# Experts' sigmoid bank and copies, layer norm sums asked two units later, last merge block on VectorE by halves

## The chip, the cores and the metric

One core of a Trainium2 chip runs the program. Its engines work side by side, each through its own queue of instructions in a fixed order: TensorE (PE, with its weight loads shown apart as PEld), VectorE (DVE), ScalarE (ACT), GpSimd (POOL) and SyncE (SP), which issues the transfers. The metric is the device time of one execution in microseconds.

## What is computed

One decoder block on 256 tokens of 1024 channels: a merge of a convolution branch and a gated linear recurrence (HGRN2), then a mixture of 32 experts of which each token takes four. Cut to what matters:

```python
mod = silu(c) @ w_ada + b_ada                       # six sections: sh1, sc1, ga1, sh2, sc2, ga2
h = rmsnorm(x, g_mix) * (1 + sc1) + sh1
p = h @ w_in                                        # 8192 columns: a, b, q, f, i, g, gc, gh
u = causal_depthwise_conv31(a * sigmoid(b)) + bias
y_conv = silu(layernorm(u, ln_g, ln_b)) @ w_conv_out
y_hg = (rmsnorm(hgrn2_scan(q, f, i)) * silu(g)) @ w_hgrn_out
merged = sigmoid(gc) * y_conv + sigmoid(gh) * y_hg
x = x + ga1 * (merged @ w_out)
h2 = rmsnorm(x, g_ffn) * (1 + sc2) + sh2
gl, lin = split(h2[tokens of e] @ w1[e] + b1[e])    # top-4 of 32 experts by the router
y = (min(gl, 7) * sigmoid(1.702 * min(gl, 7)) * (clip(lin, -7, 7) + 1)) @ w2[e] + b2[e]
out = rmsnorm(x + ga2 * sum(top_w * y), g_final)
```

## The kernel before

**Products.** The four dense products run as 44 units of 256 output columns: units 0 to 31 for w_in, 32 to 35 for w_ho (`ho_ps`), 36 to 39 for w_co (`co_ps`), 40 to 43 for w_wo (`wo_ps`). Each is 48 matmuls of 256 columns: every factor is split in a high part (rounded to the fast type) and a low part (the rest), and three of the four products are added. `split_half` (L378) makes the parts of a unit's weights in two halves of 128x1024, one unit ahead: the high part is a cast on ACT (L393), the low part a subtraction on POOL or DVE (L395, chosen by the tables SPLIT_DVE and SPLIT_HALF). Unit 31's low parts are DVE's, unit 41's are POOL's.

**Order around the units.** The loop at L711 issues unit after unit and hands out other work between them: the convolution's taps on DVE (`conv_taps`, L460, counts in the table TAPS), sections of `mod` on PE (L343, after the units in MOD_AT; a section ends in a copy to `mods` on ACT, L348), the norm of the recurrence (`oss`, `orr`, `ors`, `sg`, `o`, with casts of `sg` at L632), and the layer norm. A scheduler puts the instructions in the engines' queues. At unit LN_FROM = 23 the rest of the taps is issued and the layer norm begins; each later unit takes it a step further. Its steps: column sums `mup` of `cv` on PE (L255), copied to `mus`, totalled as `mu` (L264); `cv` minus mean on DVE (L565), squares `csq` on ACT (L569), sums `varp` (L571), copied to `vars`, totalled as `var`; reciprocal root `rv` on ACT and DVE (L229, L230), the product of `cv` with it on DVE (L579); then for 256-column pieces a sigmoid (`sigy`, L586) and an affine operation (L587) on ACT and a product on DVE (L589). In the traces a unit's matmuls are the rows `p_ps<-h,ws`, 48 of them.

**Gated merge** (L799 to L814). For each of four blocks of w_co: `tm` = `co_ps` times one gate, plus the other gate's term (both DVE, 128x512), a high part by a copy on ACT (L810), a low part by a subtraction on DVE (L811). The results `mg` are factors of w_wo's units, which start right behind.

**Experts** (L1004 on). The weights come in 1 MB loads (`w_w`) into 22 slots, issued by SP in order, each when its slot is free. An expert holds up to 64 tokens: `gather` multiplies them out into the bank `xg_ps` (L983; two experts at a time, so before every second one), `first_layer` fills the banks `u_gl` and `u_lin` (L1019, 32 matmuls of 512 columns), then gl is clamped on DVE (L1026), its sigmoid is taken on ACT (L1027), lin is clamped (L1028), and two products follow (L1029, L1030). `turn` transposes the result into the bank `ta` (L1043) and copies it out on ACT (L1045), `second_layer` multiplies by w2 into `yp` (L1058), and the results are added to `acc` (L1079). An expert with more than 64 tokens also takes a path for 32 more (`small_first`, `small_second`) behind a branch; in this input only expert 25 does. The last expert works by halves.

Of the kernel before, what the change touches and what calls it, by code (L numbers as in the profile page):

```python
# [9 lines left out]
F32 = mybir.dt.float32  # L10
# [4 lines left out]
ALU = mybir.AluOpType  # L15
PSUM = bass.MemoryType.PSUM

P = 128
# [12 lines left out]
LIMIT = 7.0  # L31
# [9 lines left out]
MOD_EXTRA = {}  # L41
LOADS = (18, 0, 0, 1, 0, 0, 1, 0, 0, 1, 0, 0, 0, 0, 1, 2, 2, 2, 2, 0, 0, 1, 0, 0, 1, 1, 0, 0, 1, 0, 0, 1, 1, 0, 0, 1, 0, 0, 0, 0, 0, 0, 0, 0, 0, 1, 0, 0, 0, 1, 1, 0, 0, 0, 0, 0, 0, 1, 1, 0, 0, 1, 1, 0, 0, 1, 0, 0, 0, 0, 0, 0, 1, 0, 0, 1, 1, 0, 0, 1, 0, 0, 0, 0, 0, 1, 0, 0, 1, 1, 0, 0, 1, 1, 2, 0, 0, 0, 0, 3, 1, 0, 0, 1, 1, 0, 0, 1, 1, 3, 0, 0, 0, 0, 0, 0, 0, 0, 0, 1, 1, 1, 0, 1, 1, 2, 0, 0, 1, 0, 0, 1, 0, 0, 1, 0, 0, 1, 1, 0, 0, 0, 0, 0, 1, 1, 0, 0, 0, 0, 1, 1, 2, 1, 0, 0, 1, 0, 0, 1, 0)
TAPS = (1, 0, 0, 0, 5, 4, 10, 6, 5, 5, 13, 6, 16, 14, 17, 11, 5, 8, 0, 6, 0, 0, 0, 0, 0, 3, 13, 9, 17, 15, 9, 5)
LN_FROM = 23
SPLIT_DVE = (3, 4, 6, 28, 29, 30, 31, 37, 38, 40, 42)
SPLIT_HALF = (4, 6, 17, 19, 21, 25, 27, 28, 32, 34, 35, 36, 40, 42, 43)
E_RUN = E
# [43 lines left out]
def block_kernel(ctx, tc, xT_d, x_d, prm_d, con_d, wada0_d, wada_d, bada_d, gfin_d, win_d, wco_d, who_d, wo_d,  # L91
                 wr_d, br_d, w1_d, b12_d, w2_d, out_d):
    nc = tc.nc
# [346 lines left out]
    def step(jobs, n):  # L440
        while n > 0 and jobs:
            try:
                next(jobs[0])
                n -= 1
            except StopIteration:
                jobs.pop(0)
# [263 lines left out]
    taps, lv0, lv1, norms, lns = [], [], [], [], []  # L710
    mods = [mod_section(j) for j in SECTIONS]  # L711
    for n, b in enumerate(IN_ORDER):
        part, i = divmod(b, 4)
        cs = slice(2 * i, 2 * i + 2)
        ps = early[n] if n < N_EARLY else block_product(n, hx, "p_ps", part == 4, n == 31)
# [54 lines left out]
        if n in MOD_AT:  # L770
            step(mods, 1)
        elif n > MOD_AT[0]:
            step(mods, MOD_EXTRA.get(n, 0))
        if n == LN_FROM:
            step(taps, 1000)
            lns.append(layer_norm())
        step(lns, 1)
        step(taps, TAPS[n])
# [6 lines left out]
    def gate(b, j):  # L785
        return gates[b // 2][:, j, b % 2 * 2:b % 2 * 2 + 2, :]

    for b in range(4):
        if b == 3:
            step(lns, 100)  # L790
        ps = block_product(32 + b, ox, "ho_ps", last=b == 3, middle=(lambda: split_y(0)) if b == 3 else None)
# [8 lines left out]
    for b in range(4):  # L800
        ps = block_product(36 + b, yx, "co_ps", last=b == 3)
        if b == 2:
            split_half(40, 0)
        if b % 2 == 0:
            mg.append(split_slot(f"mg{b // 2}"))
        tm = temp("tm").rearrange("p (m t) -> p m t", m=2)
        nc.vector.tensor_tensor(out=tm, in0=ps, in1=gate(b, 0), op=ALU.mult)
        nc.vector.tensor_tensor(out=tm, in0=tm, in1=gate(b, 1), op=ALU.add)
        hi, lo = (mg[b // 2][:, j, b % 2 * 2:b % 2 * 2 + 2, :] for j in range(2))
        nc.scalar.copy(out=hi, in_=tm)  # L810
        nc.vector.tensor_tensor(out=lo, in0=tm, in1=hi.bitcast(F32), op=ALU.subtract)  # L811
        if b % 2 == 1:
            free()
        step(preps, 2)  # L814
# [34 lines left out]
    for b in range(3):  # L849
        ps = block_product(40 + b, mg, "wo_ps", True)  # L850
# [8 lines left out]
    ps = bank("wo_ps").rearrange("p (m t) -> p m t", m=2)  # L859
# [38 lines left out]
    lo = of_rt(0, TOP_K + E)  # L898
# [9 lines left out]
    for t in range(NT):  # L908
# [4 lines left out]
                                       op0=ALU.mult, op1=ALU.add)  # L913
# [7 lines left out]
        if t == 1:  # L921
# [3 lines left out]
                                       op0=ALU.add, op1=ALU.mult)  # L925
# [81 lines left out]
    def first_layer(xg, i, w1s, hot, pieces=1):  # L1007

        up = [bank("u_gl"), bank("u_lin")]
        for nb in range(2):  # L1010
            for g in range(2):
                nc.tensor.matmul(up[nb][g * 64:(g + 1) * 64, :], lhsT=hot, rhs=b12[:, nb, g * 512:(g + 1) * 512],  # L1012
                                 start=True, stop=False)
        for kt in range(KT):
            w = w1s(kt)
            for nb in range(2):
                for g in range(2):
                    c = nb * FF + g * 512
                    nc.tensor.matmul(up[nb][g * 64:(g + 1) * 64, :], lhsT=xg[kt // 4][:, kt % 4, i * CAP:(i + 1) * CAP],  # L1019
                                     rhs=w[:, c:c + 512], start=False, stop=kt == KT - 1)  # L1020
        gl = temp("gl")
        li = temp("li")
        si = up[0]
        for c in range(0, 512, 512 // pieces):
            c = slice(c, c + 512 // pieces)
            nc.vector.tensor_scalar(out=gl[:, c], in0=up[0][:, c], scalar1=LIMIT, scalar2=None, op0=ALU.min)  # L1026
            nc.scalar.activation(si[:, c], gl[:, c], AF.Sigmoid, scale=ALPHA)  # L1027
            nc.vector.tensor_scalar(out=li[:, c], in0=up[1][:, c], scalar1=LIMIT, scalar2=-LIMIT, op0=ALU.min, op1=ALU.max)  # L1028
            nc.vector.scalar_tensor_tensor(out=li[:, c], in0=li[:, c], scalar=1.0, in1=gl[:, c], op0=ALU.add, op1=ALU.mult)  # L1029
            nc.vector.tensor_tensor(out=li[:, c], in0=li[:, c], in1=si[:, c], op=ALU.mult)  # L1030
        return li
# [6 lines left out]
    def turn(li, at_, pieces=1, piece=0):  # L1038
        ta = bank("ta")
        n = 4 // pieces  # L1040
        for j in range(piece * n, (piece + 1) * n):
            c = pick_columns(li, j) if pieces == 1 else li[:, j * P:(j + 1) * P]
            nc.tensor.transpose(ta[:, j * P:(j + 1) * P], c, ident)  # L1043
        c = slice(piece * n * P, (piece + 1) * n * P)
        nc.scalar.copy(out=at_[:, c], in_=ta[:, c])  # L1045

    def second_layer(at_, w2s, hot):
        aT = at_.rearrange("p (j g s) -> p j g s", j=4, g=2)
# [42 lines left out]
    def small_first(o, places, weights, hot, w1s, at_, owt, a, b, ps, u):  # L1091
# [17 lines left out]
        def out_of(src):  # L1109
            nc.scalar.copy(out=a[:, halves[0]], in_=src[:, halves[0]])  # L1110
            nc.vector.tensor_copy(a[:, halves[1]], src[:, halves[1]])

        out_of(ps)
        for t in range(NT):
            nc.vector.tensor_scalar(out=ow[:, t * SMALL:(t + 1) * SMALL], in0=iota[:, 0:SMALL], scalar1=places[t],
                                    scalar2=weights[t], op0=ALU.is_equal, op1=ALU.mult)
# [152 lines left out]
    for e in range(E_RUN):  # L1269
# [48 lines left out]
        at_ = li  # L1318
# [164 lines left out]
```

## Time and profile before

| | |
|---|---|
| median of 3 runs | 1324.36 us (1322.4 to 1326.33) |
| the profiled execution | 1321.67 us, its span 1319.9 us |
| PE busy | 1219.9 us, 92% of the span |
| DVE, ACT, POOL busy | 545.2, 286.5, 163.4 us |
| mean granted TensorE clock | 0.983 |
| read from HBM | 477.11 MB, 362 GB/s over the span |
| stages, from the PE timeline | w_in to 290.83, w_ho from 294.01, w_wo from 343.58, expert 0 at 384.04, expert 24 at 1068.54, expert 31 at 1282.30 |

All numbers of the trace come from the one profiled execution, in microseconds from its span's start. In a row of a timeline stand the start, the busy time, engine, line, operation, output <- inputs, the shape and the number of instructions drawn together; a bracket at the end gives the idle time of that engine just before and what ended it. "issue" is time in which the engine waited for nothing that the profile shows. PEclk is the granted clock as a share of 2.4 GHz.

### The profile page before, as it was taken

The numbers are of one execution on the slowest core, as the hardware profiler recorded it, in microseconds if no ns is written. First come the engines' busy times: TensorE is split into PE (matmuls) and PEld (weight loads), VectorE is DVE, ScalarE is ACT, GpSimd is POOL, SyncE is SP. The second block draws the span as 40 slices with busy tenths as digits, with TensorE's granted clock in tenths as the row PEclk, the third lists the DMA queues.
The fourth block names the chain that finished last, engine by engine and source line by source line (L and its number), as shares of the span: only waits on it lengthen the run. The fifth ranks groups of instructions, "written<-read, shape, count | busy, mean of one in ns | idle before, by whom it ended". The sixth has DMA issues, their size and how long they took to land. (4 is left out here: it accounts for less than half of the span.)

```text
span 1319.9 us, 19185 instructions
## 1 busy us (share of the span) xinstructions
PE 1219.9 (92%) x7829; PEld 669.9 (51%) x7829; DVE 545.2 (41%) x1121; ACT 286.5 (22%) x449; POOL 163.4 (12%) x78
## 2 busy tenths in 40 slices
PE   7999998999899999999999889988888898999997
PEld 6899788779864343443434333332323243434432
DVE  4498996545644242332323223232222232323322
ACT  4445444664720010001000000100000000100112
POOL 3258665222300000000000000000000000000000
PEclk9999989999999999999999899999999998999999
DMA  9993335656689999999999999999999999999995
GB/s 381 410 406 130 130 129 198 235 205 236 255 324 410 421 410 419 420 420 419 421 420 421 421 419 421 420 420 420 421 420 418 420 421 419 421 403 420 420 419 202
DMA packets 71399, 480.02 MB, mean 364 GB/s; under 512 B 7521, under 2 KB 8801, under 8 KB 15970
## 3 DMA queue, kind: packets, MB, share of 16 engines
q1 hardware_dynamic: 70834, 477.47, 88.5%
q8 instruction: 91, 1.49, 0.5%
q10 hardware_dynamic: 432, 0.72, 0.2%
q14 instruction: 42, 0.34, 0.1%
HBM read 477.11 MB, written 1.05 MB: 362 GB/s over the span
## 5 line engine op out<-in xcount | busy, mean ns | idle before, releaser
L1019 PE MATMUL u_gl<-w_w,xg 128*64 128x512 f32 x1024 | 270.1, 599 | 23.6 <-DMA w_w<-in_w_dram 23.6
L1019 PE MATMUL u_lin<-w_w,xg 128*64 128x512 f32 x1024 | 266.8, 592 | 0.0
L1058 PE MATMUL yp<-w_w,li 128*64 128x512 f32 x992 | 227.2, 606 | 19.1 <-ACT li L1045 10.5
L1019 PEld LDWEIGHTS u_gl<-w_w,xg 128*64 128x64 f32 x1024 | 75.9, 137 | 165.1 <-issue 88.8
L1026 DVE TENSOR_SCALAR gl<-u_gl 128x512 f32<-128x512 f32 (+1 forms) x33 | 22.3, 675 | 329.1 <-PE u_gl L1019 321.2
L1019 PEld LDWEIGHTS u_lin<-w_w,xg 128*64 128x64 f32 x1024 | 80.6, 137 | 140.0 <-issue 139.9
L1058 PEld LDWEIGHTS yp<-w_w,li 128*64 128x64 f32 x992 | 71.7, 139 | 156.5 <-issue 133.9
L409 PEld LDWEIGHTS p_ps<-h,ws 128*128 128x128 f32 x1152 | 141.4, 194 | 12.1 <-issue 5.9
L409 PE MATMUL p_ps<-h,ws 128*128 128x256 f32 x1152 | 146.2, 287 | 0.0
L1068 DVE TENSOR_TENSOR yg<-yp,ga 64x512 f32<-64x512 f32 x60 | 41.3, 689 | 225.6 <-PE yp L1058 225.0
L395 POOL TENSOR_TENSOR ws<-w_in,ws 128x1024 fp32r<-128x1024 f32 x45 | 113.1, 2527 | 87.2 <-ACT ws L393 77.8
L1276 POOL PARTITION_BROADCAST w_gfin<-w_gfin x1 | 1.3, 1305 | 898.6 <-DMA w_w<-in_w_dram 898.6
L1027 ACT ACTIVATE u_gl<-gl 128x512 f32<-128x512 f32 (+1 forms) x33 | 19.4, 589 | 427.2 <-DVE gl L1026 427.2
L460 DVE SCALAR_TENSOR_TENSOR cv<-u,pre,cv 128x229 f32<-128x229 f32 (+28 forms) x240 | 95.2, 456 | 8.6 <-ACT cv L457 7.9
L983 PE MATMUL xg_ps<-o,w_x 128*128 128x128 f32 (+1 forms) x544 | 65.4, 278 | 13.5 <-DVE li L1028 10.3
L1071 ACT ACTIVATE ys0h<-yg,by 64x512 fp32r<-64x512 f32 x30 | 21.6, 720 | 254.0 <-DVE yg L1068 254.0
L393 ACT CAST ws<-w_in 128x1024 fp32r<-128x1024 f32 x64 | 65.7, 1047 | 46.7 <-PE p_ps L409 17.6
L983 PEld LDWEIGHTS xg_ps<-o,w_x 128*128 128x128 f32 x544 | 62.2, 192 | 26.6 <-DVE li L1028 21.7
L987 DVE TENSOR_SCALAR xg<-xg_ps,g,sh 128x128 f32<-128x128 f32 (+1 forms) x136 | 45.3, 396 | 16.5 <-PE xg_ps L983 11.6
L1045 ACT COPY li<-ta 128x512 f32<-128x512 f32 (+1 forms) x33 | 18.9, 573 | 114.6 <-PE ta L1043 109.2
L395 DVE TENSOR_TENSOR ws<-w_in,ws 128x1024 fp32r<-128x1024 f32 x19 | 27.1, 1439 | 11.2 <-ACT ws L393 11.2
L409 PE MATMUL wo_ps<-ws,mg 128*128 128x256 f32 x192 | 26.0, 295 | 2.7 <-DVE mg L811 2.0
(292 smaller groups left out, 1158.1 us busy)
## 6 DMA issues: line engine op xcount, KB each, us to landing
w_w<-in_w_dram SPq DMA_DIRECT2D x380, 1024.0 KB, 19.9
w_in<-in_win_dram SPq DMA_DIRECT2D x32, 1024.0 KB, 11.0
w_ada<-in_wada_dram SPq DMA_DIRECT2D x24, 1024.0 KB, 16.3
w_ho<-in_who_dram SPq DMA_DIRECT2D x4, 1024.0 KB, 8.2
w_co<-in_wco_dram SPq DMA_DIRECT2D x4, 1024.0 KB, 8.4
w_wo<-in_wo_dram SPq DMA_DIRECT2D x4, 1024.0 KB, 9.6
w_w<-in_w_dram SPq DMA_DIRECT2D x8, 512.0 KB, 15.2
xT<-in_xT_dram SPq DMA_DIRECT2D x1, 1024.0 KB, 6.9
```

The source lines that it names most:

```text
L393: nc.scalar.copy(out=to[:, 0], in_=w[:, ks, :])
L395: (nc.vector if dve else nc.gpsimd).tensor_tensor(out=to[:, 1], in0=w[:, ks, :], in1=to[:, 0].bitcast(F32), op=ALU.subtract)
L409: nc.tensor.matmul(out, lhsT=lt, rhs=rh, start=first and kt == 0 and i == 0, stop=kt == KT - 1 and i == 2, skip_group_check=not first)
L460: nc.vector.scalar_tensor_tensor(out=cv[:, ct, s:], in0=u[i][:, m, :T - s], scalar=tap, in1=cv[:, ct, s:], op0=ALU.mult, op1=ALU.add)
L983: nc.tensor.matmul(ps[:, i, cs], lhsT=x2[:, t, kt * P:(kt + 1) * P], rhs=o[:, 0, t, cs], start=t == 0, stop=t == NT - 1)
L987: nc.vector.tensor_scalar(out=xg[h][:, i, cs], in0=ps[:, i, cs], scalar1=g2[:, kt:kt + 1], scalar2=sh2[:, kt:kt + 1], op0=ALU.mult, op1=AL ...
L1019: nc.tensor.matmul(up[nb][g * 64:(g + 1) * 64, :], lhsT=xg[kt // 4][:, kt % 4, i * CAP:(i + 1) * CAP], rhs=w[:, c:c + 512], start=False, s ...
L1026: nc.vector.tensor_scalar(out=gl[:, c], in0=up[0][:, c], scalar1=LIMIT, scalar2=None, op0=ALU.min)
L1027: nc.scalar.activation(si[:, c], gl[:, c], AF.Sigmoid, scale=ALPHA)
L1058: nc.tensor.matmul(yp[g * 64:(g + 1) * 64, :], lhsT=aT[:, kt % 4, kt // 4, :], rhs=w[:, kk, g * 512:(g + 1) * 512], start=False, stop=kt = ...
L1068: nc.vector.tensor_tensor(out=y[rows, :], in0=yp[gs, :], in1=ga2[gs, :], op=ALU.mult)
L1071: nc.scalar.activation(hi[rows, :], y[rows, :], AF.Copy, scale=by[rows, :])
```

## The change

Three independent parts. First, a constant TAPS_END = 23 keeps the place at which the taps are issued, and LN_FROM moves from 23 to 25, so that the layer norm's steps are asked two units later. Second, the fourth block of the gated merge is done in two halves of 256 columns, and its high part is copied by DVE; the other blocks stay. Third, in the experts: the sigmoid is written to the bank of `u_lin` in place of that of `u_gl`, with lin's clamp issued ahead of it; the copy out of `ta` is two copies of 256 columns; and the first copy of `small_first` is one copy of 512 columns on ACT in place of one half on ACT and one on DVE.

```diff
@@ -41,7 +41,8 @@
-LN_FROM = 23
+TAPS_END = 23
+LN_FROM = 25
 SPLIT_DVE = (3, 4, 6, 28, 29, 30, 31, 37, 38, 40, 42)
 SPLIT_HALF = (4, 6, 17, 19, 21, 25, 27, 28, 32, 34, 35, 36, 40, 42, 43)
 E_RUN = E
@@ -771,8 +772,9 @@
             step(mods, 1)
         elif n > MOD_AT[0]:
             step(mods, MOD_EXTRA.get(n, 0))
+        if n == TAPS_END:
+            step(taps, 1000)
         if n == LN_FROM:
-            step(taps, 1000)
             lns.append(layer_norm())
         step(lns, 1)
         step(taps, TAPS[n])
@@ -804,11 +806,16 @@
         if b % 2 == 0:
             mg.append(split_slot(f"mg{b // 2}"))
         tm = temp("tm").rearrange("p (m t) -> p m t", m=2)
-        nc.vector.tensor_tensor(out=tm, in0=ps, in1=gate(b, 0), op=ALU.mult)
-        nc.vector.tensor_tensor(out=tm, in0=tm, in1=gate(b, 1), op=ALU.add)
         hi, lo = (mg[b // 2][:, j, b % 2 * 2:b % 2 * 2 + 2, :] for j in range(2))
-        nc.scalar.copy(out=hi, in_=tm)
-        nc.vector.tensor_tensor(out=lo, in0=tm, in1=hi.bitcast(F32), op=ALU.subtract)
+
+        for m in (slice(0, 1), slice(1, 2)) if b == 3 else (slice(0, 2),):
+            nc.vector.tensor_tensor(out=tm[:, m], in0=ps[:, m], in1=gate(b, 0)[:, m], op=ALU.mult)
+            nc.vector.tensor_tensor(out=tm[:, m], in0=tm[:, m], in1=gate(b, 1)[:, m], op=ALU.add)
+            if b == 3:
+                nc.vector.tensor_copy(hi[:, m], tm[:, m])
+            else:
+                nc.scalar.copy(out=hi[:, m], in_=tm[:, m])
+            nc.vector.tensor_tensor(out=lo[:, m], in0=tm[:, m], in1=hi[:, m].bitcast(F32), op=ALU.subtract)
         if b % 2 == 1:
             free()
         step(preps, 2)
@@ -1020,12 +1027,13 @@
                                      rhs=w[:, c:c + 512], start=False, stop=kt == KT - 1)
         gl = temp("gl")
         li = temp("li")
-        si = up[0]
+
+        si = up[1]
         for c in range(0, 512, 512 // pieces):
             c = slice(c, c + 512 // pieces)
             nc.vector.tensor_scalar(out=gl[:, c], in0=up[0][:, c], scalar1=LIMIT, scalar2=None, op0=ALU.min)
+            nc.vector.tensor_scalar(out=li[:, c], in0=up[1][:, c], scalar1=LIMIT, scalar2=-LIMIT, op0=ALU.min, op1=ALU.max)
             nc.scalar.activation(si[:, c], gl[:, c], AF.Sigmoid, scale=ALPHA)
-            nc.vector.tensor_scalar(out=li[:, c], in0=up[1][:, c], scalar1=LIMIT, scalar2=-LIMIT, op0=ALU.min, op1=ALU.max)
             nc.vector.scalar_tensor_tensor(out=li[:, c], in0=li[:, c], scalar=1.0, in1=gl[:, c], op0=ALU.add, op1=ALU.mult)
             nc.vector.tensor_tensor(out=li[:, c], in0=li[:, c], in1=si[:, c], op=ALU.mult)
         return li
@@ -1041,8 +1049,10 @@
         for j in range(piece * n, (piece + 1) * n):
             c = pick_columns(li, j) if pieces == 1 else li[:, j * P:(j + 1) * P]
             nc.tensor.transpose(ta[:, j * P:(j + 1) * P], c, ident)
-        c = slice(piece * n * P, (piece + 1) * n * P)
-        nc.scalar.copy(out=at_[:, c], in_=ta[:, c])
+
+        for j in range(piece * n, (piece + 1) * n, 2):
+            c = slice(j * P, (j + 2) * P)
+            nc.scalar.copy(out=at_[:, c], in_=ta[:, c])
 
     def second_layer(at_, w2s, hot):
         aT = at_.rearrange("p (j g s) -> p j g s", j=4, g=2)
@@ -1110,7 +1120,8 @@
             nc.scalar.copy(out=a[:, halves[0]], in_=src[:, halves[0]])
             nc.vector.tensor_copy(a[:, halves[1]], src[:, halves[1]])
 
-        out_of(ps)
+
+        nc.scalar.copy(out=a, in_=ps)
         for t in range(NT):
             nc.vector.tensor_scalar(out=ow[:, t * SMALL:(t + 1) * SMALL], in0=iota[:, 0:SMALL], scalar1=places[t],
                                     scalar2=weights[t], op0=ALU.is_equal, op1=ALU.mult)
```

Lines of the changed kernel are up to ten further down: L255 is L256, L586 is L587, L811 is L818, L1045 is L1055.

PE's queue around units 24 to 27, before: `p_ps` rows are the units (two rows each), `ob` belongs to the recurrence, `mod` to the modulation.

```order
L609 MATMUL ob<-at_1164,v 128x128
L255 MATMUL mup<-cv,pre 32x256 x8
L409 MATMUL p_ps<-h_150,ws 128x256 x24
L409 MATMUL p_ps<-h_151,ws 128x256 x24
L607 MATMUL ob<-at_1164,v 128x256
L609 MATMUL ob<-at_1164,v 128x128
L607 MATMUL ob<-at_1164,v 128x256
L609 MATMUL ob<-at_1164,v 128x128
L264 MATMUL mu<-mus,con 128x256
L409 MATMUL p_ps<-h_150,ws 128x256 x24
L409 MATMUL p_ps<-h_151,ws 128x256 x24
```

After, units 24 to 26 and the start of 27:

```order
L410 MATMUL p_ps<-h_150,ws 128x256 x24
L410 MATMUL p_ps<-h_151,ws 128x256 x24
L608 MATMUL ob<-at_1682,v 128x256
L610 MATMUL ob<-at_1682,v 128x128
L608 MATMUL ob<-at_1682,v 128x256
L610 MATMUL ob<-at_1682,v 128x128
L344 MATMUL mod_2112<-w_ada_2_2057,pre 32x512 x4
L256 MATMUL mup<-cv,pre 32x256 x8
L410 MATMUL p_ps<-h_150,ws 128x256 x24
L410 MATMUL p_ps<-h_151,ws 128x256 x24
L608 MATMUL ob<-at_1682,v 128x256
L610 MATMUL ob<-at_1682,v 128x128
```

`mup` stood ahead of unit 24 and stands ahead of unit 26; `mu`, ahead of unit 25 before, now stands ahead of unit 27 (behind the last rows shown). Likewise `varp` moves from unit 26 into unit 28 and `var` from ahead of unit 27 to ahead of unit 29, and the last two sections of `mod`, which stood ahead of and behind unit 31, both stand ahead of it.

ACT's queue ahead of unit 31, before; `w_in_2762` is the weight of unit 30, `w_in_2808` that of unit 31, `gates` rows close a unit, `o_3195` are the casts of `sg`.

```order
L586 ACTIVATE sigy<-cv,pre 128x256 x2
L587 ACTIVATE cv<-cv,pre 128x256 x2
L586 ACTIVATE sigy<-cv,pre 128x256 x2
L587 ACTIVATE cv<-cv,pre 128x256 x2
L374 COPY ga_181<-bb 128x512
L764 ACTIVATE gates<-p_ps 128x512
L632 CAST o_3124<-sg 128x512 x2
L393 CAST ws<-w_in_2762 128x1024 x2
L764 ACTIVATE gates<-p_ps 128x512
L632 CAST o_3195<-sg 128x512
L393 CAST ws<-w_in_2808 128x1024
L632 CAST o_3195<-sg 128x512
```

After; `w_in_2793` is the weight of unit 31, `gates` at the top closes unit 29, at the bottom unit 30.

```order
L765 ACTIVATE gates<-p_ps 128x512
L587 ACTIVATE sigy<-cv,pre 128x256 x2
L633 CAST o_3171<-sg 128x512 x2
L588 ACTIVATE cv<-cv,pre 128x256 x2
L587 ACTIVATE sigy<-cv,pre 128x256 x2
L588 ACTIVATE cv<-cv,pre 128x256 x2
L587 ACTIVATE sigy<-cv,pre 128x256 x2
L588 ACTIVATE cv<-cv,pre 128x256 x2
L587 ACTIVATE sigy<-cv,pre 128x256 x2
L588 ACTIVATE cv<-cv,pre 128x256 x2
L394 CAST ws<-w_in_2793 128x1024 x2
L765 ACTIVATE gates<-p_ps 128x512
```

The sixteen operations on `sigy` and `cv` stood ahead of unit 30's casts; now they and two casts of `sg` stand between unit 30's casts and those of unit 31.

DVE's queue at the last block of the merge, before:

```order
L811 TENSOR_TENSOR mg_3807<-tm,mg_3807 128x512
L395 TENSOR_TENSOR ws<-w_wo_3322,ws 128x1024
L807 TENSOR_TENSOR tm<-co_ps,gates 128x512
L808 TENSOR_TENSOR tm<-tm,gates 128x512
L811 TENSOR_TENSOR mg_3807<-tm,mg_3807 128x512
L845 TENSOR_TENSOR tmo<-wo_ps,ga_3331 128x256
L846 TENSOR_TENSOR w_x<-w_x,tmo 128x256
```

After:

```order
L818 TENSOR_TENSOR mg_3807<-tm,mg_3807 128x512
L396 TENSOR_TENSOR ws<-w_wo_3322,ws 128x1024
L812 TENSOR_TENSOR tm<-co_ps,gates 128x256 x2
L813 TENSOR_TENSOR tm<-tm,gates 128x256 x2
L815 CAST mg_3807<-tm 128x256 x2
L818 TENSOR_TENSOR mg_3807<-tm,mg_3807 128x256 x2
L852 TENSOR_TENSOR tmo<-wo_ps,ga_3331 128x256
L853 TENSOR_TENSOR w_x<-w_x,tmo 128x256
```

Three operations of 512 columns became eight of 256, the copy `CAST` among them, which ACT's queue loses. POOL and SP keep their instructions in their order.

## Rows read from the trace of the kernel before

**Rows 1.** The page, GB/s moved in 40 equal slices of the span

```profile
GB/s 381 410 406 130 130 129 198 235 205 236 255 324 410 421 410 419 420 420 419 421 420 421 421 419 421 420 420 420 421 420 418 420 421 419 421 403 420 420 419 202
```

**Rows 2.** Waits of PE weight loads, 410 to 1066 us: total, times, longest

```profile
PEld u_gl L1019 <- DMA w_w<-in_w_dram: 65.2, 58, 1.8
```

**Rows 3.** Timeline of PE, experts 24 and 31

```profile
1083.34 1.08 PE L1019 MATMUL u_gl<-w_w,xg 128*64 128x512 f32 x4 [0.55 <-DMA w_w<-in_w_dram]
...
1093.72 9.36 PE L1058 MATMUL yp<-w_w,li 128*64 128x512 f32 x30 [3.58 <-issue]
...
1296.83 1.03 PE L1019 MATMUL u_gl<-w_w,xg 128*64 128x512 f32 x4
```

**Rows 4.** Windows: busy time (operations) of each engine, granted clock, DMA share, GB/s

```profile
262.10:270.10 8.00, 8.00 (x54) 5.36 (x53) 4.23 (x5) 7.99 (x18) 0.00 (x0) 1.00 0.81 339
350.00:355.00 5.00, 3.73 (x20) 3.74 (x21) 2.37 (x4) 0.28 (x1) 3.44 (x2) 0.66 1.02 431
405.00:410.00 5.00, 4.80 (x24) 1.66 (x26) 0.62 (x2) 0.14 (x1) 0.00 (x0) 1.00 0.94 356
475.00:480.00 5.00, 4.21 (x26) 2.08 (x23) 2.66 (x4) 0.60 (x1) 0.00 (x0) 1.00 0.95 349
1165.00:1170.00 5.00, 4.32 (x21) 2.43 (x21) 2.83 (x7) 1.19 (x2) 0.00 (x0) 1.00 0.80 305
1304.00:1305.00 1.00, 0.87 (x4) 0.30 (x5) 0.00 (x0) 0.85 (x2) 0.00 (x0) 1.00 0.13 49
```

**Rows 5.** Timeline of PE, units 23 to 31

```profile
220.75 0.64 PE L255 MATMUL mup<-cv,pre 128*32 128x256 f32 x2 [3.65 <-DVE cv L460]
221.32 7.46 PE L409 MATMUL p_ps<-h,ws 128*128 128x256 f32 x48
...
239.85 2.09 PE L571 MATMUL varp<-csq,pre 128*32 128x256 f32 x12 [0.44 <-ACT csq L569]
...
251.28 0.70 PE L264 MATMUL var<-vars,con 128*128 128x256 f32 x2
...
292.60 1.98 PE L367 MATMUL gb<-mods,con 128*128 128x512 f32 x4 [0.71 <-ACT mods L348]
```

**Rows 6.** Timeline of ACT, ahead of the unit 30 casts

```profile
270.99 1.14 ACT L632 CAST o<-sg 128x512 fp32r<-128x512 f32 x2
```

**Rows 7.** Timeline of DVE, layer norm

```profile
255.62 2.28 DVE L579 TENSOR_TENSOR cv<-cv,rv 128x2048 f32<-128x2048 f32 x1
257.82 1.22 DVE L395 TENSOR_TENSOR ws<-w_in,ws 128x1024 fp32r<-128x1024 f32 x1
```

**Rows 8.** Timeline of all engines, last block of the merge and w_wo

```profile
342.43 0.69 DVE L811 TENSOR_TENSOR mg<-tm,mg 128x512 fp32r<-128x512 f32 x1
...
343.58 4.48 PE L409 MATMUL wo_ps<-ws,mg 128*128 128x256 f32 x36
...
345.15 0.68 DVE L807 TENSOR_TENSOR tm<-co_ps,gates 128x512 f32<-128x512 f32 x1
...
348.31 5.14 POOL L395 TENSOR_TENSOR ws<-w_wo,ws 128x1024 fp32r<-128x1024 f32 x2 [9.94 <-ACT ws L393]
...
348.78 2.43 DVE L811 TENSOR_TENSOR mg<-tm,mg 128x512 fp32r<-128x512 f32 x1 [2.21 <-ACT mg L810]
...
348.80 0.50 PE L409 MATMUL wo_ps<-ws,mg 128*128 128x256 f32 x2 [0.74 <-ACT mg L810]
...
351.26 8.56 PE L409 MATMUL wo_ps<-ws,mg 128*128 128x256 f32 x58 [1.96 <-DVE mg L811]
```

**Rows 9.** Timelines of PE and ACT, experts 27 and 31

```profile
1191.47 3.84 PE L983 MATMUL xg_ps<-o,w_x 128*128 128x128 f32 x32 [0.78 <-DVE li L1028]
...
1196.68 7.09 PE L1058 MATMUL yp<-w_w,li 128*64 128x512 f32 x32 [0.34 <-ACT li L1045]
...
1196.04 0.59 ACT L1045 COPY li<-ta 128x512 f32<-128x512 f32 x1 [4.85 <-PE ta L1043]
...
1301.37 0.37 ACT L1045 COPY li<-ta 128x256 f32<-128x256 f32 x1
```

## The prediction

> **What bounds the kernel now.** I read four views in this order: the page's slices, the waits of PE, the windows, then the timelines of the stretches that the diff touches. The slices show a transfer rate of about 420 GB/s from the thirteenth slice to the last but one, with one lower slice [rows 1]: while the experts run, the 1 MB weight loads fill the DMA engines. The waits say that PE follows that stream: between 410 and 1066 us its weight loads waited 58 times, 65.2 us together, for w_w [rows 2]. The stream is started by PE, which frees the slots that the next loads want. So whatever comes off the front end (everything ahead of expert 0, which starts at 384 us) moves the whole stream and the end with it, while time saved inside the first 24 experts is given back as a longer wait for weights.
>
> This changes late. The last first-layer tile of expert 24 still waits 0.55 us for DMA; then come a pause of 3.58 us and the overflow work of expert 25, and PE no longer meets a late weight [rows 3]. From about 1084 us PE's own chain bounds. How far may it speed up before the weights bound again? The last load lands near 1304.5 us (49 GB/s in the microsecond before 1305, [rows 4]). The eight half-megabyte loads behind the last first-layer tile are 4.19 MB, 10 us at 420 GB/s, so that tile lands near 1294.6 (an estimate from these two); PE uses it at 1296.83 [rows 3]. The cover is 2.2 us.
>
> So there are two kinds of currency: PE time in the front end counts in full; expert time counts after 1084 us, up to 2.2 us and whatever the stream itself gains.
>
> **Layer norm sums, two units later.** Before, PE asks for mup right after unit 23, when the conv taps on DVE are not done: it waits 3.65 us, and unit 24 behind it takes 7.46 us for 48 matmuls [rows 5], where 36 elsewhere take 4.48 [rows 8], that is 6.0 for 48: 1.4 lost to a cold stretch. varp waits 0.44 for the squares, and gb waits 0.71 for mods, whose last section stands behind unit 31 [rows 5]. After, the taps have two units of cover, and the last two mods sections stand ahead of unit 31, so all four go: 3.65 + 1.4 + 0.44 + 0.7 = 6.2 us.
>
> What is late next is ACT. Its 16 sigmoid and affine operations filled the 8 us from 262.1 to 270.1 (18 operations with two others, ACT busy 7.99, [rows 4]), 7.9 us without the others, ten us ahead of the unit 31 casts. Now they stand between unit 30's casts and unit 31's, with two casts of sg (1.0 us, [rows 6]) among them, and PE cannot start unit 31 without the casts. Counting from the end of unit 29: var's sum is asked just ahead of unit 29; before, the product cv*rv on DVE ended at 257.9 [rows 7], 6.6 us behind var's start at 251.28 [rows 5]; after, rv stands behind a cast that waits for PE's ors and DVE, so I lay it at 8.5, which puts the first sigmoid 2.5 us behind unit 29's end. Then 7.9 + 1.0 of ACT work and a cast of 1.05: the first half of unit 31's high part is there 12.5 us behind unit 29's end. PE meanwhile does ors (1.3), unit 30 (6.0) and mods (1.8, sized by the like operations before): 9.1. It waits 3.4, and another 1.0 for the low part, which is a subtraction of 1.22 us on DVE [rows 7]: 4.5. The cover that hides it otherwise is PE's own nine microseconds. Gain 6.2 - 4.5 = 1.7 if unit 31 runs warm, 0.3 if it loses 1.4 as unit 24 did. I take **1.0**. From both sides: with rv only 6.6 behind var the wait falls to 2.6 and the gain is 3.6; if ACT is held 2.5 longer it is a loss of 1.5. POOL and SP have the same instructions in the same order, so no transfer's place in its queue moves.
>
> **The gated merge.** Before, wo's unit 40 issues 36 matmuls, waits 0.74 for ACT's copy, issues two, waits 1.96 for DVE's subtraction, and then 58 take 8.56 us at a granted clock of 0.66 between 350 and 355 [rows 4, 8], that is the lower level of 1.2 GHz for a part of it; at 0.125 each they would take 7.2. The copy was late because it stood behind three copies and a cast on ACT. The subtraction took 2.43 us where the same operation took 0.69 six microseconds earlier; POOL's split began at 348.31, 0.47 us ahead of it [rows 8]. After, DVE does multiply, add, copy and subtract in eight half operations, from 345.15. A full one takes 0.68 [rows 8], so a half takes 0.35 to 0.45 and the eight end between 348.0 and 348.7, against the 348.06 at which PE arrives. Unit 40 then ends near 349.6. Next is unit 41, whose first low part is POOL's first split, half of the row of 5.14 us: done near 350.9. PE waits 1.2, runs 48 warm, and reaches 356.9 where it was 359.66 before: **2.8**. Low end 1.4, if the stretch is cold again; high end 3.2, if hi-only pairs cover part of the wait.
>
> A rule speaks against the edit. The trace shows 2.43 us against 0.69 for the same subtraction with POOL at work. The Trainium skill, "SBUF — State Buffer", section "Who interferes with whom", says that a VectorE operation with both inputs in SBUF and a GpSimd operation that reads SBUF share a port pair that one holds for its whole instruction, and whoever issues first wins. The rows agree: the subtraction ended at 351.2, just behind POOL's first split. By that rule the last half subtraction, if it starts behind 348.31, again ends near 351 and the gain is about 2.5; since PE awaits the same split anyway, the sum hardly changes.
>
> **The experts.** Three edits. The sigmoid goes into the u_lin bank, so the u_gl bank is free once gl is read, and the next gather of odd experts, which takes that bank, no longer waits 0.78 for DVE's li [rows 9]. In even experts the sigmoid now stands behind the clamp, at most 0.1 later at the last multiply. The copy of ta by halves lets the first yp start after 0.37 instead of 0.59 us [rows 9], where PE now waits 0.34 for it: 0.22 an expert. The ACT copy in the overflow path replaces an ACT and a DVE half: about 0.2, once. In the first 24 experts PE waits for weights, so these count only where the stream sags because PE frees slots late: 405 to 410 us (356 GB/s, 0.8 us lost) and 475 to 480 (349, 0.8), [rows 4]. I take **1.0** of these 1.6; 0 and 1.4 are the ends. From 1084 us on they count directly: 7 x 0.22 + 2 x 0.78 + 0.2 = 3.3. The cap is the cover of 2.2 and what the sag from 1165 to 1170 (305 GB/s, 1.4 us lost, [rows 4]) gives back, up to 1.0. I take **2.7**; 1.0 to 3.3.
>
> **Sum.** 1.0 + 2.8 + 1.0 + 2.7 = 7.5 us. The profiled execution took 1321.67 us, its span 1319.9, so 1.8 lie around the span; it would take 1314.2. The median of the runs is 1324.36, 2.7 above the profiled one; less 7.5 it is **1316.9**. A measurement of this kernel can tell about 0.3%, 4 us, from no change.
>
> **Rivals.**
> A, as summed, 1313 to 1320: chance 0.55.
> B, the ACT queue ahead of unit 31 is longer than I laid out, the wait there 7 and not 4.5: the layer norm loses 1.5 in place of gaining 1.0, total 5.0, 1319.4. For it: ACT's new order puts a cast of sg, which waits for PE and DVE, ahead of rv. Chance 0.14.
> C, no wait ahead of unit 31, the whole 6.2 stays: total 12.7, 1311.7. It needs the sigmoids to run in gaps that ACT's 7.9 us do not leave beside unit 30 alone. Chance 0.09.
> D, the experts' edits are hidden: behind the pause at 1093 the stream stays the bound, the sags stay, and the merge is cold again: 1.0 + 1.4 = 2.4, 1322.0, no measurable change. For it: the cover is only 2.2 us and was worked out from two estimates. Chance 0.16.
> E, slower. Two matmuls into expert 24's second layer PE stands still for 3.58 us, released by nothing that the profile shows ("issue", [rows 3]), and the 30 matmuls behind it take 9.36 us, where 32 take 7.09 [rows 9], so 2.7 more: 6.3 each. Ahead of 1084 us the stream hides most of such a pause; behind it nothing does. If the shifted timing puts two more of them there, it is +12.6 - 7.5 = +5.1, 1329.5. It decides from two extra pauses on; one still leaves a gain of 1.2. Against it: only one lies behind 1080 us. Chance 0.06.
>
> **Numbers.** Faster by over 0.3%: A, B, C, 0.78. Within: D, 0.16. Slower: E, 0.06. The range runs from C's time, with the bounds of the wait, to D's: 1311.5 to 1322.0; about 0.18 is left out, E and the outer halves of C and D.
>
> **What would show it.** Right: no PE wait at mup; a wait of 3 to 5 us ahead of unit 31 released by ACT's casts or DVE's low part; gates (L764 before) of unit 30 late on ACT; ho_ps starting near 293; no wait for mg in wo, one of about 1 us for POOL's ws; expert 0 near 380; no wait of xg_ps for li in odd experts; yp waiting about 0.1 for ACT. The step from 384 to the last stream byte should be the same or 1 us shorter. Wrong: PE still waiting for mup, or for varp by microseconds; mg still the releaser in wo; a DMA wait of first-layer tiles returning behind expert 26, which would mean that the cover was smaller than 2.2; or new "issue" pauses behind 1084 us.

## The result, and the profile after

The changed kernel took 1315.19 us (median of 7 runs, 1314.48 to 1320.1) against 1324.36 (7 runs, 1322.22 to 1327.14): a ratio of 0.9939 with a 95% interval of 0.9925 to 0.9954. The profiled execution took 1317.53 us, its span 1315.9. A later trace of the same kernel, `after_again`, has a span of 1313.1; what lies between the two is told below. Each trace is of one execution; line numbers of the kernels that were run differ by a few from one to the next.

**Ahead of unit 31.** PE's timeline of the changed kernel, from unit 30's end to w_ho (the columns as in [rows 5]):

```profile
275.30 1.92 PE L344 MATMUL mod<-w_ada,pre 128*32 128x512 f32 x14
280.66 0.73 PE L410 MATMUL p_ps<-h,ws 128*128 128x256 f32 x2 [3.45 <-ACT ws L394]
281.92 8.24 PE L410 MATMUL p_ps<-h,ws 128*128 128x256 f32 x46 [0.53 <-DVE ws L396]
290.00 1.88 PE L368 MATMUL gb<-mods,con 128*128 128x512 f32 x4
291.31 8.96 PE L410 MATMUL ho_ps<-o,ws 128*128 128x256 f32 x70
```

None of the three waits of [rows 5] (for the taps, the squares and `mods`) is left; in their place PE waits 3.45 us for ACT's cast of unit 31 and 0.53 for DVE's low part. Behind them 46 matmuls take 8.24 us, 0.18 each against 0.125. The windows of the same trace (columns as in [rows 4]) show the granted clock there, and around expert 0, the second place where it fell:

```profile
280.00:284.00 4.00, 2.81 (x11) 2.52 (x12) 2.80 (x4) 4.00 (x6) 0.94 (x1) 0.59 0.59 224
284.00:288.00 4.00, 4.00 (x22) 4.00 (x22) 2.52 (x1) 1.45 (x2) 1.72 (x2) 0.55 0.74 262
372.00:377.00 5.00, 4.40 (x32) 3.49 (x31) 4.51 (x30) 1.59 (x3) 0.00 (x0) 0.93 1.00 423
377.00:383.00 6.00, 6.00 (x24) 3.75 (x25) 1.75 (x8) 0.00 (x0) 0.00 (x0) 0.50 0.26 109
```

The granted clock is 0.59 and 0.55, near the lower level of 1.2 GHz, behind the wait; and 0.50 from 377 to 383 us, where the router's short gaps lie just ahead.

**The merge.** All engines, last block (before: [rows 8]):

```profile
344.19 0.75 DVE L818 TENSOR_TENSOR mg<-tm,mg 128x256 fp32r<-128x256 f32 x2
...
345.61 4.93 POOL L396 TENSOR_TENSOR ws<-w_wo,ws 128x1024 fp32r<-128x1024 f32 x2 [9.95 <-ACT ws L394]
...
348.04 5.90 PE L410 MATMUL wo_ps<-ws,mg 128*128 128x256 f32 x47 [1.12 <-POOL ws L396]
...
348.64 2.18 DVE L853 TENSOR_TENSOR w_x<-w_x,tmo 128x256 f32<-128x256 f32 x1
```

The subtractions end 0.7 us before POOL's split begins, and PE's one wait is 1.12 us for that split. From the first matmul of w_wo to the first transpose behind its second unit it is 12.90 us; it was 16.09.

**The end.** PE's timeline in expert 31, and the only DMA wait line of PE behind 1084 us:

```profile
1277.86 1.08 PE L1026 MATMUL u_gl<-w_w,xg 128*64 128x512 f32 x4 [0.47 <-DMA w_w<-in_w_dram]
...
1292.76 1.08 PE L1026 MATMUL u_gl<-w_w,xg 128*64 128x512 f32 x4 [0.58 <-DMA w_w<-in_w_dram]
```

```profile
PE u_gl L1026 <- DMA w_w<-in_w_dram: 3.0, 7, 0.6
```

Before, PE waited for no first-layer tile of expert 31 ([rows 3] shows the last); now it waits for four of them, the last one at 1292.76. The stream of weights bounds the kernel up to that tile; behind it the second layer of expert 31 meets no late weight, and PE's own chain takes it to the end.

### The profile page after: what moved, and what is told of

It reads as the page before. It is cut to its first block, busy times and chain, and to the rows that moved or that the text cites. A ratio compares the mean times of both kernels' runs of the same rounds, so it can differ in the third digit from the quotient of the medians.

```text
span 1315.9 us, 19280 instructions
## 1 busy us (share of the span) xinstructions
PE 1220.0 (93%) x7829; PEld 670.7 (51%) x7829; DVE 541.7 (41%) x1125; ACT 287.9 (22%) x479; POOL 161.6 (12%) x78
## 5 line engine op out<-in xcount | busy, mean ns | idle before, releaser
L1068 PE MATMUL yp<-w_w,li 128*64 128x512 f32 x992 | 221.5, 599 | 6.7 <-issue 2.9
L410 PEld LDWEIGHTS p_ps<-h,ws 128*128 128x128 f32 x1152 | 143.4, 196 | 14.5 <-ACT ws L394 6.6
L1036 ACT ACTIVATE u_lin<-gl 128x512 f32<-128x512 f32 (+1 forms) x33 | 19.4, 589 | 445.8 <-DVE li L1035 445.7
L990 PE MATMUL xg_ps<-o,w_x 128*128 128x128 f32 (+1 forms) x544 | 71.1, 291 | 16.5 <-issue 13.9
L990 PEld LDWEIGHTS xg_ps<-o,w_x 128*128 128x128 f32 x544 | 67.9, 205 | 29.5 <-issue 14.6
L994 DVE TENSOR_SCALAR xg<-xg_ps,g,sh 128x128 f32<-128x128 f32 (+1 forms) x136 | 45.3, 395 | 26.4 <-PE xg_ps L990 15.4
L1055 ACT COPY li<-ta 128x256 f32<-128x256 f32 x64 | 20.8, 375 | 97.1 <-PE ta L1051 93.5
L1082 DVE SCALAR_TENSOR_TENSOR ys0l<-yg,by,ys0h 64x512 fp32r<-64x512 f32 x30 | 22.4, 748 | 13.5 <-ACT ys0h L1081 12.6
## 6 DMA issues: line engine op xcount, KB each, us to landing
w_in<-in_win_dram SPq DMA_DIRECT2D x32, 1024.0 KB, 11.1
```

The costliest lines, as they stand in the source:

```text
L410: nc.tensor.matmul(out, lhsT=lt, rhs=rh, start=first and kt == 0 and i == 0, stop=kt == KT - 1 and i == 2, skip_group_check=not first)
L990: nc.tensor.matmul(ps[:, i, cs], lhsT=x2[:, t, kt * P:(kt + 1) * P], rhs=o[:, 0, t, cs], start=t == 0, stop=t == NT - 1)
L994: nc.vector.tensor_scalar(out=xg[h][:, i, cs], in0=ps[:, i, cs], scalar1=g2[:, kt:kt + 1], scalar2=sh2[:, kt:kt + 1], op0=ALU.mult, op1=AL ...
L1068: nc.tensor.matmul(yp[g * 64:(g + 1) * 64, :], lhsT=aT[:, kt % 4, kt // 4, :], rhs=w[:, kk, g * 512:(g + 1) * 512], start=False, stop=kt = ...
L1082: nc.vector.scalar_tensor_tensor(out=lo[rows, :], in0=y[rows, :], scalar=by[rows, :], in1=hi[rows, :].bitcast(F32), op0=ALU.mult, op1=ALU. ...
```

## The experiments

One table for all traces, my own sums of rows: w_wo's first matmul to the first transpose behind its second unit (wo), from there to expert 1 (e1), expert 1 to the last weight's landing (stream), from that to the end (lag), and where the last PE pause of over 2 us stands that ends with no release in the profile. The column us is the time of the one profiled execution.

| kernel | us | wo | e1 | stream | lag | last pause at |
|---|---|---|---|---|---|---|
| before | 1321.67 | 16.09 | 52.5 | 891.7 | 16.0 | 1093.7, yp, expert 24 |
| after | 1317.53 | 12.90 | 55.5 | 892.6 | 14.0 | 1059.9, xg_ps, expert 23 |
| after_again | 1314.80 | 12.88 | 52.3 | 893.8 | 14.0 | 1056.7, xg_ps, 23 |
| ln_only | 1324.74 | 16.22 | 55.8 | 893.1 | 15.4 | 1097.5, yp, 24 |
| merge_only | 1320.72 | 12.90 | 52.5 | 894.4 | 16.1 | 1092.6, yp, 24 |
| experts_only | 1323.97 | 16.23 | 55.5 | 892.9 | 14.0 | 1065.6, xg_ps, 23 |
| no_bank | 1315.15 | 12.91 | 52.2 | 893.4 | 14.0 | 1057.0, xg_ps, 23 |
| no_turn | 1313.40 | 12.91 | 52.5 | 892.4 | 14.0 | 1059.3, xg_ps, 23 |
| small_only | 1320.92 | 16.25 | 52.5 | 892.5 | 14.0 | 1064.0, xg_ps, 23 |
| bank_only | 1324.36 | 16.23 | 55.8 | 892.8 | 14.9 | 1098.0, yp, 24 |
| ln24 | 1313.72 | 12.89 | 55.5 | 892.9 | 14.0 | 1056.0, xg_ps, 23 |
| sig_late | 1310.56 | 12.90 | 52.2 | 892.6 | 14.0 | 1052.5, xg_ps, 23 |
| warm | 1309.49 | 12.90 | 52.8 | 893.2 | 14.0 | 991.7, ta, 21 |
| warm_only | 1320.56 | 16.23 | 53.0 | 893.0 | 14.3 | 1064.9, xg_ps, 23 |

**The three parts alone, and all of them again.** Each is the kernel before with one part of the diff (TAPS_END and LN_FROM = 25; the merge; the three edits in the experts); the fourth is the changed kernel once more.

> The layer norm part alone; merge and experts as before. Theory (each part counts by itself: front-end time moves the stream and the end): w_ho starts about 2 us earlier than in the kernel before, counted from unit 23's end, with a wait of about 4 us ahead of unit 31, and the median is 1 to 3 us below the kernel before. Rival (front-end gains are lost again in a cold stretch of PE at expert 0, as the profile after shows, so only the experts' edits are seen at the end): no difference, within 1 us.

> The merge part alone. Theory: the stretch from the start of w_wo to its second unit's end is 3 us shorter, PE's only wait there is about 1 us for POOL's split, and the median is 2.5 to 3.5 us below the kernel before. Rival (lost in the cold stretch at expert 0): no difference, within 1 us.

> The experts' three edits alone. Theory: the last weight lands up to 1 us earlier, and the distance from its landing to the end, 16 us before, shrinks by about 2 us, since PE reaches the end of the stream with no lag: the median is 2 to 4 us below the kernel before. Rival (the front end's gains are lost and these edits carry all of it): 8 to 9 us below.

> The changed kernel once more, for a second trace and a time beside the three parts. Theory: about 9 us below the kernel before, the sum of the three parts within 2 us; and if the cold stretch at expert 0 is a matter of chance, an execution near 1314.5 us shows expert 0's first matmuls at full clock and its first yp 3 us earlier than the trace after. Rival (the cold stretch belongs to the changed kernel): the same granted clock below 1 between 374 and 384 us in this trace too.

Against a median of 1325.31 for the kernel before (29 runs): ln_only 1322.12 (ratio 0.9979, 0.9966 to 0.9992), merge_only 1319.67 (0.9964, 0.9948 to 0.9980), experts_only 1321.98 (0.9973, 0.9960 to 0.9987), after_again 1314.57 (0.9925, 0.9905 to 0.9944). As ratios the parts give -2.8, -4.8 and -3.6 us, 11.1 together, against -9.9 for the whole with 2.6 either way. The sum and the whole agree within the noise, each part's interval lies below 1, and the rival that the experts carry all of it fell. Two details of the theories missed: merge_only came out below its 2.5 to 3.5 us (the interval reaches 2.7, the stretch itself is 3.2 shorter), and in experts_only the last weight did not land earlier (the stream took 892.9 us against 891.7). In ln_only the wait ahead of unit 31 is the same (3.45 and 0.76), in merge_only the wait for POOL is (1.13). after_again differs from after mainly at expert 0 (e1 is 3.3 us shorter; unit 31 lost 1.2 less to the clock, and the stream took 1.2 longer); its windows:

```profile
372.00:377.00 5.00, 4.39 (x36) 3.72 (x35) 4.77 (x29) 0.86 (x3) 0.00 (x0) 1.00 1.00 421
377.00:383.00 6.00, 6.00 (x33) 2.32 (x34) 1.18 (x5) 0.00 (x0) 0.00 (x0) 1.00 0.47 169
```

PE is as busy in the first stretch (4.39 of 5 us against 4.40), yet the clock stays at 1.00. The cold stretch is no fixed property of the changed kernel.

**The wait ahead of unit 31.** Two kernels on top of the changed one:

```diff
# sig_late
-        step(lns, 1)
+        if n != 29:
+            step(lns, 1)
# ln24
-LN_FROM = 25
+LN_FROM = 24
```

> The changed kernel with the layer norm's last step (sigmoids, affine operations, their product) asked one unit later, behind unit 30 in place of unit 29, so that unit 31's casts stand ahead of most of it on ACT. Theory (the wait ahead of unit 31 is ACT's queue and nothing else): no wait over 1 us ahead of unit 31, unit 31 warm in about 6 us in place of 9.5, w_ho starts 5 to 6.5 us earlier than in the changed kernel, and the median is 4 to 6 us below the changed kernel, near 1309.5. Rival (the casts of w_ho, which now stand behind the sigmoids, are the next to be late): the wait moves ahead of w_ho's first unit with 3 us or more, and the median is within 2 us of the changed kernel.

> The changed kernel with the layer norm's sums asked one unit earlier, behind unit 24. Theory: mup finds the taps done with no wait; the sixteen operations now stand ahead of unit 30's casts and hold them by 2 to 3 us in place of unit 31's 4, so w_ho starts 0 to 2 us earlier than in the changed kernel and the median is 0 to 2 us below it. Rival (one unit is enough for both, the taps and ACT): no wait at either place, 5 us below the changed kernel.

sig_late: 1310.46 us (ratio to the kernel before 0.9896, 0.9874 to 0.9917), 4.1 below after_again's median, and 4.4 and 4.7 below no_bank and no_turn (told below), which were run beside it and keep the wait. PE around unit 31:

```profile
276.57 1.06 PE L344 MATMUL mod<-w_ada,pre 128*32 128x512 f32 x6
277.56 6.01 PE L410 MATMUL p_ps<-h,ws 128*128 128x256 f32 x48
283.51 1.06 PE L344 MATMUL mod<-w_ada,pre 128*32 128x512 f32 x8
286.23 1.98 PE L368 MATMUL gb<-mods,con 128*128 128x512 f32 x4 [1.66 <-ACT mods L349]
287.65 12.55 PE L410 MATMUL ho_ps<-o,ws 128*128 128x256 f32 x100
```

No wait ahead of unit 31, and the unit in 6.01 us. From the first `ob` behind unit 23 to w_ho it takes 72.6 us, against 77.5 in after and 76.5 in after_again: 3.9 to 4.9 less, just short of the 5 to 6.5 expected. A smaller wait of 1.66, for ACT's copy of mods behind the sigmoids, is what is late next. ln24: 1312.26 us (0.9906, 0.9885 to 0.9927), 2.3 below after_again and 2.6 to 2.9 below no_bank and no_turn beside it; its one wait of PE between units 24 and 31 is 0.21 us for the squares, and the same stretch takes 73.3 us. The waits are as the rival said and not as the theory did: with the sums one unit later than before the taps are done, and the sixteen operations, which then stand ahead of unit 30's casts, do not hold them. The time lies between the two (0 to 2 us, and 5), and its one trace holds the cold stretch at expert 0. By the waits, two units were one too many.

**The experts' edits: what they cost, and what moved.** no_bank and no_turn are the changed kernel with the sigmoid back in u_gl's bank, or with one copy out of ta; small_only and bank_only are the kernel before with one edit:

```diff
# small_only
-        out_of(ps)
+        nc.scalar.copy(out=a, in_=ps)
# bank_only
-        si = up[0]
+        si = up[1]
```

(bank_only has the clamp of lin ahead of the sigmoid too.)

> The changed kernel with the sigmoid back in the u_gl bank. Theory (behind 1084 us PE now has more reserve than the weights' stream allows to use): xg_ps waits 0.8 for li in odd experts again, yet the distance from the last weight's landing to the end stays near 14.0 us and the median stays within 1 us of the changed kernel. Rival (each saved wait counts at the end): 1.6 us above the changed kernel, the distance 15.5.

> The changed kernel with one copy of 512 columns out of ta again. Theory: yp waits 0.34 for ACT in each expert again, yet the distance from the last weight's landing to the end stays near 14.0 us and the median within 1 us of the changed kernel. Rival (each saved wait counts at the end): 1.5 us above it, the distance 15.5.

> The kernel before with one edit, the first copy of the overflow path as one ACT copy. Theory (what shortened the end is the place of PE's last long pause with no release: in expert 24's second layer in every trace without the experts' edits, in expert 23's gather in every trace with them): this edit, common to all kernels whose pause moved, moves it too, the distance from the last weight's landing to the end falls from 16.0 to 14.0 us, and the median is about 2 us below the kernel before, although the edit's own saving is 0.2. Rival (each edit is worth its own saving): the pause stays in expert 24, the distance stays at 15.8, no difference in the median.

> The kernel before with the sigmoid in the u_lin bank, nothing else. Theory: the pause stays in expert 24; the waits of xg_ps for li go in odd experts, 0.78 each, of which two lie behind expert 24: the distance from the last landing to the end is 14.5 us, the median 1 to 2 us below the kernel before. Rival (this edit moves the pause): the pause in expert 23 or earlier, the distance 14.0.

no_bank 1314.82 us (0.9933, 0.9908 to 0.9957) and no_turn 1315.14 (0.9938, 0.9915 to 0.9961), against after_again's 1314.57 (0.9925): no difference that can be told, but these intervals of 6 us could not tell 0 from the rivals' 1.5 either. The traces decide. Their waits behind 1084 us are back, in no_bank and in no_turn:

```profile
PE xg_ps L990 <- DVE li L1035: 1.6, 2, 0.8
```

```profile
PE yp L1066 <- ACT li L1053: 2.4, 7, 0.3
```

and the lag is 14.0 in both, not 15.5. So the waits were rightly priced and are covered. Small_only shows by what: an edit priced at 0.2 us gives 1321.53 (0.9977, 0.9964 to 0.9990), 3 us, and the lag of 14.0. The pause of 3.58 us of [rows 3] has left the stretch behind 1084 us. The rows of the pauses, of bank_only and of small_only:

```profile
1097.96 7.53 PE L1059 MATMUL yp<-w_w,li 128*64 128x512 f32 x24 [3.95 <-issue]
```

```profile
1063.99 1.57 PE L983 MATMUL xg_ps<-o,w_x 128*128 128x128 f32 x11 [2.86 <-issue]
```

bank_only, 1323.01 us (0.9978, 0.9967 to 0.9990), keeps the pause in expert 24, and its lag is 14.9, not the 14.5 expected: shorter by 1.1 where two waits of 0.78 went (the pause itself was 0.4 longer). With the pause in expert 23, PE waits for weights again behind it and the lag is 14.0 to 14.3 in every trace; with one of 3.6 to 4 us in expert 24 it is 14.9 to 16.1.

Two limits of this. Ln_only, experts_only, small_only, bank_only and warm_only all lie 2.8 to 3.6 us below the kernel before, so the times do not tell these causes apart; the lag does. And small_only's trace holds a second difference: the 64 overflow matmuls of expert 25 take 8.1 us there, at a granted clock of 1.00, where they take 9.8 at 0.83 in all five traces without the overflow path's edit (with it, 8.1 in six traces and 9.5 in three). That this is not what shortens the lag shows in warm_only, which has none of the experts' edits: its overflow path takes 9.8, its last pause is in expert 23, and its lag is 14.3.

**The cold stretch.** Eight dummy matmuls of 128 columns, four ahead of the last transposes and two ahead of each of the router's counts, on top of sig_late and on top of the kernel before:

```diff
+    fb = bank("fb")[:, 0:P]
+    def warm_up(n):
+        for _ in range(n):
+            nc.tensor.matmul(fb, lhsT=ident, rhs=ident, start=True, stop=True)
+    warm_up(4)
     route_part(3, (1,))
...
+        warm_up(2)
         nc.tensor.matmul(pc[:, t, :], lhsT=tri, rhs=sel[:, t, :], start=t == 0, stop=True)
```

> The kernel sig_late with eight dummy matmuls of 128 columns in the gaps in which PE waits for the router ahead of expert 0. Theory (the spread between executions is a fall of the granted clock to half around expert 0, after these gaps, in some executions and not in others): the clock stays at 1.00 there in more executions, the runs lie closer together, and the median is 1 to 2 us below sig_late. Rival (the fall doesn't come from these gaps): the same spread of 4 to 5 us, the median the same or up to 1 us above.

> The kernel before with nothing but the eight dummy matmuls in PE's gaps ahead of expert 0. Theory (most executions of the kernel before lose about 3 us to a stretch at half the granted clock around expert 0, which its one trace happens not to show, and the gaps bring it): the trace shows the clock at 1.00 from 366 to 390 us, expert 0 begins within 1 us of the kernel before, and the median is 2 to 3 us below the kernel before. Rival (dummy work ahead of the gather only delays it, and the spread has another source): the median the same or up to 1 us above, the same spread.

warm: 1309.82 us (0.9885, 0.9868 to 0.9902), five runs from 1308.25 to 1310.96; sig_late's six from 1308.76 to 1313.47. It is the fastest kernel here, though not measurably faster than sig_late, so this run decides between theory and rival no further. warm_only: 1320.61 us (0.9975, 0.9962 to 0.9988), 3.3 below the kernel before, its runs within 4.4 us where the 17 of the kernel before beside it lie within 7.9. Its clock stayed whole behind the gaps, as the theory said:

```profile
374.00:382.00 8.00, 7.75 (x59) 6.48 (x57) 6.38 (x39) 3.20 (x9) 0.00 (x0) 1.00 1.01 425
382.00:390.00 8.00, 8.00 (x48) 3.70 (x49) 2.02 (x9) 0.00 (x0) 0.00 (x0) 1.00 0.50 207
```

against bank_only, without dummies:

```profile
374.00:382.00 8.00, 6.76 (x47) 5.22 (x47) 6.21 (x40) 3.83 (x11) 0.00 (x0) 1.00 0.97 406
382.00:390.00 8.00, 8.00 (x33) 4.44 (x34) 2.17 (x9) 0.00 (x0) 0.00 (x0) 0.57 0.26 108
```

One trace shows little here, since seven of the twelve traces without dummies keep the clock at expert 0 too; the narrower spread is the better sign. And the dummies also moved the last pause out of expert 24 (table), which is worth up to 1.8 us of lag. How much of the 3.3 is the clock is therefore not separated by this run.

## Why the prediction was right, step by step

The forecast was 1316.9 from a sum of 7.5 us; the ratio gives 8.1 (6.1 to 9.9), the two medians differ by 9.2. That the sum came so close is in part luck: by the traces the layer norm and the merge gave 2.3 us more than forecast, and the stream and the end 3.7 less.

**What bounds.** Right, and more so than I used it. The change saved expert time: even experts went from 25.39 to 25.18 us, odd ones from 27.59 to 26.73: the 0.2 of the copies, and 0.65 of the gathers' 0.78. Expert 25 went from 47.7 to 46.0 in after, where its overflow matmuls ran at full clock, and to 47.1 in after_again, where they did not. That is 3 to 4 us behind 1084, more than could be used. With the pause gone as well PE caught up with the weights, and the cap of 2.2, worked out from two rows of before, set the gain: the lag fell from 16.0 to 14.0. One sign that was to mean "wrong" came with it: first-layer tiles wait for DMA again behind expert 26, 2.9 us in experts 30 and 31 of after. It means that the cover was used up, not that it was smaller than 2.2 by much: the lag fell by 2.1. I put this term at 2.7, with up to 1.0 from a stream that would itself gain.

**The sags.** Here the step failed: I took 1.0 us for sags in the stream that faster experts would fill. From expert 1 to the last landing it is 891.7 us before and 892.4 to 894.4 in all other traces; nothing was gained, and the trace of before was the shortest of all. Two of the sags of [rows 4] did shrink in after: from 349 to 408 GB/s in the window from 475 us, and from 305 in that from 1165 to 393 in that from 1160. But the first grew: from 405 to 410 us the rate was 356 GB/s before and 282 in after, and in after_again it was 313 and then 351 from 400 to 410. Why is open. A transfer rate that reads 420 in nearly every window does not show whether a gap can be had.

**Layer norm.** The three waits went and so did unit 24's cold stretch; 3.4 + 1.0 was forecast for the new wait, from durations of before alone, and 3.45 + 0.53 to 0.76 measured. I gave it 1.0 us, between warm and cold; it was cold (unit 31 lost 3.0 us in after and 1.7 in after_again, not 1.4), and still the stretch from the first ob behind unit 23 to w_ho fell from 79.4 to 77.5 in after, 76.5 in after_again and 77.7 in ln_only: 1.7 to 2.9. Waits and cold units nearly cancel: the waits of that stretch sum to 4.8 us in before and 4.2 in after_again, and unit 24 lost 1.5 where unit 31 lost 1.7. The size was missed because varp and mup, no longer split by a wait, took 1.5 us less than before (2.3 against 3.1, and 1.0 against 1.7 busy), which I did not count; most of the rest is 0.55 less in the 52 matmuls of `mod`. Other traces with the old order take 78.6 to 80.7 us for the stretch, so the trace of before is not the longest, and the gain may be larger than these three pairs say. Rivals B and C both fell.

**Merge.** 2.8 forecast, 3.2 measured in every trace that has it. The 1.2 us for POOL's split was 1.12; the eight half operations took 2.5 us, 0.3 each and not 0.35 to 0.45, so that DVE was through ahead of POOL and the rule of the Trainium skill, "SBUF — State Buffer", "Who interferes with whom", did not come to bear at this place. It fits one step on: the addition to w_x, two inputs in SBUF, took 2.18 us and ended 0.3 behind POOL's second split, where its like takes 0.42 alone, as the rule has it; nobody waited for it.

**Rival E**, pauses of 3.58 us that fall somewhere else, was the right mechanism with the wrong sign. The edits did move the pause: out of the stretch where it costs, not into it. Its price was off as well: I gave a pause 6.3 us, and its going took 2 us off the lag, since PE then meets the stream.

**Where the rest of the medians' difference comes from.** Between two traces that both lack the cold stretch, before and after_again, the spans differ by 6.8 us: 2.9 layer norm, 3.2 merge, 0.2 in expert 0, 2.1 lag, 0.5 ahead of unit 23, less 2.1 that the stream took longer. The medians differ by more. Of the 29 runs of the kernel before beside the three parts, four took 1320.8 to 1322.0 at a mean granted clock of 0.984 to 0.986, and 25 took 1323.8 to 1327.7 at 0.978 to 0.983; its trace, at 1321.67 and 0.983, is by its time one of the few. Of 13 runs of the changed kernel nine took 1313.3 to 1315.2. That the larger part of the runs of before holds the cold stretch of 3 us, and fewer runs of the changed kernel do, fits these numbers and is argued, not shown; there is no trace of a late run of before. The traces with one part or one edit fit it too: ln_only, experts_only and bank_only, profiled at 1324.0 to 1324.7, hold the stretch; merge_only, small_only and warm_only, at 1320.6 to 1320.9, do not.

## To carry to other kernels

When a wait is moved off by asking for a sum later, write down what the same queue does next and by when the next consumer wants it; here a sum over one unit's steps showed both, and by ln24's waits one unit of delay would have been enough. Take the slack between the stream and the engine as the cap of every saving behind the point where the engine takes over: of the three edits in the experts the smallest alone brought the lag to its floor of 14.0, and leaving out either of the others took nothing away. And compare traces only after looking at the granted clock slice by slice: one execution is not the median.

## What had not been expected

PE's long pauses that the profile puts to "issue" seem to go by the program more than by the run: all four traces without the overflow path's edit and without dummies have the last one of over 2 us in expert 24's second layer, all others have it earlier, mostly at expert 23's gather, though small_only adds no PE instruction. The one kernel with two traces shows how far this goes: after and after_again share three such places, but after alone has one of 2.88 us at 667.7, and after_again alone a shorter one, of 1.76, in expert 24. In the traces before, after, after_again and small_only a 16 KB packet of the instruction queue moves in each of the 14 pauses over 2 us behind 380 us (one of them, in before, is put to PE's sequencer), or at its very start. The queue's line for 1090 to 1094 us of before and for 1055 to 1060 us of after:

```profile
q8 instruction: 1, 0.02, 1.7%
```

```profile
q8 instruction: 1, 0.02, 1.3%
```

There are 63 such packets between 380 and 1320 us of before, one in 15 us, and most of them meet no pause. That PE waits for its instructions is likely from this, not shown.

And the clock: the same short gaps ahead of expert 0 (0.63, 0.30 and 0.17 us in all twelve traces without dummies) are followed by 6 to 7 us at half the clock in five of the twelve and by no fall in the other seven. What decides between the two is open. The cost is 3.3 us of the e1 column, like with like, and since the front end sets the start of the weights' stream, it reaches the end: the stream column is no shorter behind it (892.6 to 893.1 us in the five, 891.7 to 894.4 in the others).
